# Two-layer hybrid decoder in fp32: the end of the last up unit ahead of the down units' preparation, and other tiles for their raw weights

## The chip, the cores and the metric

The kernel runs on one core of one Trainium2 chip. The metric is the device time of one execution, in microseconds. The core's engines are named as the profile names them: PE is TensorE (matmuls), PEld its weight loads, DVE is VectorE, ACT is ScalarE, POOL is GpSimd, SP is the engine whose queue issues the weight loads.

## The reference

Activations are 512 tokens by 1024 features; the feed-forward part is 2816 wide (22 chunks of 128).

```
def swiglu(x, w_gate, w_up, w_down):
    return (jax.nn.silu(x @ w_gate) * (x @ w_up)) @ w_down

h = x
for i in range(2):
    # layer 0: h = h + conformer_conv(rms_norm(h));  layer 1: h = h + diff_attention(rms_norm(h))
    u = rms_norm(h, ffn_norm_g[i])
    h = h + swiglu(u, ffn_w_gate[i], ffn_w_up[i], ffn_w_down[i])
    gate = jax.nn.sigmoid(rms_norm(h, ple_norm_g[i]) @ ple_w_gate[i])
    h = h + gate * (p[i] @ ple_w_proj[i])
return h
```

## The kernel before

Everything is kept transposed: `h[c]` holds feature chunk c (128 partitions) for the 512 tokens. Each fp32 product is made of three matmuls on rounded parts (`mm3`: L166 low times high, L167 high times high, L168 high times low). So each operand is split: ScalarE casts it to its high part, VectorE subtracts that from it for the low part. Weights come by DMA on SP's queue into a raw tile and are split in the same way.

The feed-forward function `ffn` goes through its 22 hidden chunks in three parts (6, 8, 8). In the second and third part the gate, up and down products are done by units (`Unit`, with `Gate`, `Up`, `Down`): a unit makes a 256-wide piece of output with seven products of half size instead of eight, each product `p(i)` being 12 matmuls 256 wide. For it a unit needs two raw weight tiles (`load`), sums and differences of their quarters on GpSimd (in `prep(1)`: L739, L740; in `prep(3)`: L751, L752), and their splits (`two`: cast L729, low part L730; the third sum: L755, L756). `drain` takes finished accumulators: L784, L790 and L795 add them up, L816 and L821 multiply up by gate, and L823 and L824 split the hidden chunk into the tile `B{chunk}`. `run` goes through a list of units: while unit n multiplies, unit n+1 is loaded and prepared.

The last eight hidden chunks go through `down`. Output chunks 0 and 1 are done plainly (512-wide matmuls into two accumulators, all chunks one after another), output chunks 2 to 7 by three `Down` units 0, 1, 2. These need differences of the hidden chunks as second operands. They are made out of the up units' results (L830 to L833: on GpSimd, for the last up unit on VectorE) into the tiles C and D, which otherwise hold `pp`, the projected per-layer input, and are split by `sums(k)` (L927 cast, L928 low part). When they have been read, `back` loads `pp` into these tiles again (L954). `add` (L920) adds a finished accumulator to `h`; when a chunk of `h` is finished, `after.chunk(m)` prepares the next norm: split (L206 on ScalarE, L207 on VectorE), square (L225, L228), sum of squares on GpSimd (L229). The gate after it (`ple`) needs the sum over partitions (L199, on TensorE), an inverse root, and its spreading by a matmul (L291) and copy (L262); then L1020 multiplies the gate's accumulator by it, which frees that accumulator.

The order on each engine is set by a tile scheduler that builds the program: it knows the data that each instruction needs and where a tile's buffer comes free, and `tc.issue_after` adds that an instruction is put behind a given one. Tiles are named by tag and count of buffers: `sb([P, 2, S], "A4", 1)` is the one buffer A4, "wraw" has two buffers. A tile with the same tag can be written only when the one before is no longer read.

In a Down unit before the change, raw tiles of unit 0 are in A4, A5, of unit 1 in A6, A7, of unit 2 in "wraw"; its sums are in A2, A3, A4, the third sum in "wth".

Of the kernel before, what the change touches and what calls it, by code (L numbers as in the profile page):

```python
# [15 lines left out]
ALU = mybir.AluOpType  # L16
# [4 lines left out]
P = 128  # L21
S = 512
# [69 lines left out]
def trunk(ctx, tc, xT, pT, wts, diag, dww, vec, rel, onehot, lamv, out):  # L92
    nc = tc.nc
# [45 lines left out]
    t = tp()  # L139
# [69 lines left out]
    class Norm:  # L209


        def __init__(self, g, acc_engine=None):
            self.g, self.u = g, {}
            self.eng = acc_engine or G
# [592 lines left out]
    class Up(Unit):  # L807
# [4 lines left out]
        def ready(self, j, k):  # L812
            o, g = self.out[j], self.gate.out[j]
            cut = slice(k * HT, (k + 1) * HT)
            if j == 1:
                V.tensor_tensor(o[:, cut], self.a[:, :HT] if k == 0 else o[:, cut], g[:, cut], ALU.mult)  # L816
            self.done[j] += 1
            if self.done[j] < 2:
                return
            if j == 0:  # L820
                V.tensor_tensor(o, o, g, ALU.mult)  # L821
            hid = both(sb([P, 2, S], f"B{self.at + j}", 1, F32R))
            A.copy(hid[0], o)  # L823
            V.tensor_tensor(hid[1], o, f(hid[0]), ALU.subtract)  # L824
            self.hid[self.at + j] = hid
            if self.pp and self.done == [2, 2]:
                (u11, u12), (u21, u22) = ((u[:, :HT], u[:, HT:]) for u in self.out)
                t = [x[:, i * HT : (i + 1) * HT] for x in self.pp[self.at : self.at + 2] for i in range(2)]
                eng = G if self.at + 2 < len(self.hid) else V
                eng.tensor_tensor(t[0], u12, u11, ALU.subtract)  # L830
                eng.tensor_tensor(t[1], u22, t[0], ALU.subtract)
                eng.tensor_tensor(t[2], u22, u12, ALU.subtract)
                eng.tensor_tensor(t[3], u21, t[1], ALU.subtract)  # L833

    class Down(Unit):
        def __init__(self, n, m, b, add, done):
            super().__init__(n, False, None)
            self.m, self.b, self.add, self.done = m, b, add, done

        def load(self):  # L840
            self.raw = []
            for j in range(2):
                raw = sb([P, 2, S], *(("wraw", 2) if self.n == 2 else (f"A{4 + 2 * self.n + j}", 1)))
                nc.sync.dma_start(raw, wts[self.i + j].rearrange("p (j k) -> p j k", j=2))
                self.raw.append(raw)
            self.sums = sb([P, 2, S], f"A{2 + self.n}", 1)
            self.s3 = sb([P, S], "wth", 2)

        def third(self):
            return sb([P, S], "wtl", 2, F32R), sb([P, S], "bias", 2, F32R)  # L850
# [14 lines left out]
    def ffn(norm, after, spare, pp, pps):  # L865
# [11 lines left out]
                x.b = ops.at  # L877
            return us

        def run(us, between=lambda: None):  # L880
            for n, x in enumerate(us):
                if n == len(us) - 1:
                    between()
                last = us[n - 1] if n else None
                nxt = us[n + 1] if n + 1 < len(us) else None
                x.start()
                if nxt:
                    nxt.load()
                x.p(1)
                if nxt:  # L890
                    nxt.prep(0)
                x.p(2)
                if nxt:
                    nxt.prep(1)
                if last:
                    last.p(4)
                x.p(6)
                if nxt:
                    nxt.prep(2)
                if last:  # L900
                    last.p(3)
                x.p(5)
                if nxt:
                    nxt.prep(3)
                    nxt.prep(4)
                x.p(7)
                if nxt:
                    nxt.prep(5)
            us[-1].p(4)
            us[-1].p(3)  # L910

        def down(hid):

            ws = [weight(), weight()]
            b = {n: [None] * 4 for n in ("T1", "T2", "T3", "T4")}
# [3 lines left out]
            def add(m, cut, src):  # L919
                V.tensor_tensor(h[m][:, cut], src, h[m][:, cut], ALU.add)  # L920

            def sums(k):
                hi, lo = ops.tiles[k]
                for i in range(2):
                    two = slice(2 * i, 2 * i + 2)
                    src = pp[2 * k + i].rearrange("p (j t) -> p j t", j=2)
                    A.copy(hi[:, two], src)  # L927
                    V.tensor_tensor(lo[:, two], src, f(hi[:, two]), ALU.subtract)  # L928
                for i in range(4):
                    b[f"T{i + 1}"][k] = hi[:, i], lo[:, i]  # L930

            xs = [Down(i, 2 * i + 2, b, add, after.chunk) for i in range(3)]
            x = xs[0]
            x.load()
            x.prep(0)
            x.prep(1)
            for k in range(3):
                sums(k)
            x.prep(3)
            sums(3)  # L940
            x.prep(2)
            x.prep(4)
            accs = mm(), mm()
            for k in range(NC):
                for w_, a_ in zip(ws, accs):
                    mm3(a_, wpart(w_, k), hid[k], k == 0, k == NC - 1)
            for m in range(2):
                add(m, slice(0, S), accs[m])
                after.chunk(m)
            x.prep(5)  # L950

            def back():
                for m in range(NC):
                    nc.sync.dma_start(pp[m], pps[m])  # L954

            run(xs, back)

        us = None
        for at, (f0, n) in enumerate(PARTS):
# [42 lines left out]
            if hooks:  # L1002
                linear(n, hid, add, 2, at=hooks)
                wnext[0] = end
            else:
                down(hid)

    def ple(norm, pp, after, last_cuts=1):
        def sums(m, cuts=1):
# [504 lines left out]
```

## Time and profile before

| | us |
|---|---|
| median of 3 runs | 1272.56 (1271.6 to 1272.82) |
| the profiled execution | 1272.05 |
| its span | 1270.3 |
| layer 0's last up unit and first down unit | about 490 to 536 in the span |
| layer 1's | about 1147 to 1193 |
| the gate after each | begins with L199 at 575.5, and its first accumulator is freed at 585.7 and 1243.5 |

In a row of the timeline stand the start in the span, the time of the instruction, its engine, its line, what it writes and reads by tags, and its shape; in brackets, how long the engine had been idle before and what ended that. Matmuls overlap, so their pitch is the difference of two starts. In the rows of windows stand, for a stretch, its length and the busy time of PE, PEld, DVE, ACT and POOL with the counts, then the granted clock of TensorE (1 is full), the share of the DMA engines that is busy, and GB/s.

### The profile page before, as it was taken

How to read it: one execution, taken by the hardware profiler on the slowest of the kernel's cores; microseconds unless marked ns; L12 is line 12 of the kernel's file. 1: busy time of each engine (PE TensorE's matmuls, PEld its weight loads, DVE VectorE, ACT ScalarE, POOL GpSimd, SP SyncE). 2: the span in 40 equal slices, each digit the busy share in tenths (PEclk: the TensorE clock that was granted, in tenths of full speed). 3: DMA queues.
4: the chain of work that ended last, by engine and by line, in shares of the span. 5: the costliest groups of instructions: out<-in, count | busy, mean ns of one | idle time of the engine just before them, and what ended most of it. 6: DMA issues, size and time to landing. Idle time of an engine off the chain costs nothing.

```text
span 1270.3 us, 19093 instructions
## 1 busy us (share of the span) xinstructions
PE 1239.8 (98%) x7296; PEld 1092.9 (86%) x7296; DVE 937.8 (74%) x1308; ACT 639.3 (50%) x1124; POOL 544.6 (43%) x403
## 2 busy tenths in 40 slices
PE   9999999999999999799999999999999999999798
PEld 7888778889998999697788888888889998999787
DVE  6997866975895488877676876647956984597866
ACT  6652554533553355344666877644434542455332
POOL 3862432025550577523346635141035541696330
PEclk9999999999999999899999999999999999999799
DMA  7556323333333234234442331343243233234132
GB/s 263 187 202 190 125 87 112 92 108 116 100 98 119 83 101 129 87 93 142 125 126 78 101 101 58 102 132 99 83 133 100 88 113 116 84 100 151 50 98 85
DMA packets 53768, 144.79 MB, mean 114 GB/s; under 512 B 6147, under 2 KB 10755, under 8 KB 53676
## 3 DMA queue, kind: packets, MB, share of 16 engines
q1 hardware_dynamic: 50400, 138.04, 34.9%
q10 hardware_dynamic: 3276, 5.53, 1.4%
q8 instruction: 57, 0.93, 0.3%
q14 instruction: 35, 0.29, 0.1%
HBM read 133.04 MB, written 10.51 MB: 113 GB/s over the span
## 4 chain that ended last, share of the span: by engine, by line
PE 81%; DVE 9%; issue 3%; DMA 1%; ACT 1%; SPq 0%; POOL 0%; ACTq 0%; DVEq 0%
PE mm L166 25%; PE mm L168 25%; PE mm L167 25%; DVE wlo L730 2%; PE mm L1225 1%; DVE sc L458 1%; DVE B L824 1%; DVE C L928 1%; PE sc L1193 1%; PE sc L1192 1%; PE tp L1212 1%; PE sc L407 1%; DVE wk L816 1%; PE mm L407 1%; PE mm L363 1%
## 5 line engine op out<-in xcount | busy, mean ns | idle before, releaser
L159 ACT CAST whi<-wraw 128x1024 fp32r<-128x1024 f32 (+2 forms) x133 | 133.1, 1009 | 185.6 <-PE mm L168 71.8
L166 PE MATMUL mm<-A,wlo 128*128 128x512 f32 (+1 forms) x568 | 220.4, 389 | 2.4 <-DVE big L1020 1.9
L167 PE MATMUL mm<-A,whi 128*128 128x512 f32 (+1 forms) x568 | 218.9, 387 | 0.0
L168 PE MATMUL mm<-A,whi 128*128 128x512 f32 (+1 forms) x568 | 217.3, 389 | 0.0
L161 DVE TENSOR_TENSOR wlo<-wraw,whi 128x1024 fp32r<-128x1024 f32 (+2 forms) x129 | 167.6, 1304 | 61.3 <-ACT whi L159 58.8
L166 PE MATMUL mm<-C,wlo 128*128 128x256 f32 x520 | 147.9, 285 | 1.9 <-DVE h L920 1.9
L167 PE MATMUL mm<-C,whi 128*128 128x256 f32 x520 | 147.7, 284 | 0.0
L168 PE MATMUL mm<-C,whi 128*128 128x256 f32 x520 | 147.7, 284 | 0.0
L730 DVE TENSOR_TENSOR wlo<-A,whi 128x1024 fp32r<-128x1024 f32 x74 | 123.2, 1672 | 19.8 <-ACT whi L729 19.3
L166 PE MATMUL mm<-B,wlo 128*128 128x512 f32 (+1 forms) x328 | 123.1, 375 | 12.0 <-ACT B L823 8.3
L166 PEld LDWEIGHTS mm<-A,wlo 128*128 128x128 f32 x568 | 106.8, 188 | 26.3 <-DVE big L1020 2.7
L168 PEld LDWEIGHTS mm<-A,whi 128*128 128x128 f32 x568 | 106.4, 188 | 22.1 <-DVE A L620 0.7
L167 PEld LDWEIGHTS mm<-A,whi 128*128 128x128 f32 x568 | 106.9, 188 | 21.0
L168 PE MATMUL mm<-B,whi 128*128 128x512 f32 (+1 forms) x328 | 120.8, 374 | 1.8 <-DVE B L824 1.8
L167 PE MATMUL mm<-B,whi 128*128 128x512 f32 (+1 forms) x328 | 122.5, 373 | 0.0
L229 POOL TENSOR_TENSOR acc<-acc,wk 128x512 f32<-128x512 f32 x35 | 55.4, 1584 | 151.1 <-ACT wk L228 150.5
L729 ACT CAST whi<-A 128x1024 fp32r<-128x1024 f32 x74 | 77.3, 1048 | 67.4 <-PE mm L168 51.8
L739 POOL TENSOR_TENSOR A<-A 128x512 f32<-128x512 f32 x20 | 31.2, 1560 | 172.6 <-DMA A<-in_wts 171.9
L166 PEld LDWEIGHTS mm<-C,wlo 128*128 128x128 f32 x520 | 100.3, 193 | 3.0 <-DVE h L920 2.7
L167 PEld LDWEIGHTS mm<-C,whi 128*128 128x128 f32 x520 | 100.3, 193 | 0.2
L168 PEld LDWEIGHTS mm<-C,whi 128*128 128x128 f32 x520 | 100.3, 193 | 0.0
L739 POOL TENSOR_TENSOR A<-wraw 128x512 f32<-128x512 f32 x18 | 30.8, 1709 | 149.3 <-DMA wraw<-in_wts 139.8
(341 smaller groups left out, 3196.9 us busy)
## 6 DMA issues: line engine op xcount, KB each, us to landing
wraw<-in_wts SPq DMA_DIRECT2D x153, 512.0 KB, 3.6
A<-in_wts SPq DMA_DIRECT2D x40, 512.0 KB, 3.5
wraw<-in_wts SPq DMA_DIRECT2D x16, 384.0 KB, 3.1
D<-in_diag SPq DMA_DIRECT2D x22, 256.0 KB, 4.9
C<-in_diag SPq DMA_DIRECT2D x16, 256.0 KB, 4.8
C<-pp SPq DMA_DIRECT2D x10, 256.0 KB, 2.6
h<-in_xT SPq DMA_DIRECT2D x8, 256.0 KB, 5.1
rest<-h SPq DMA_DIRECT2D x8, 256.0 KB, 2.0
```

The costliest lines, as they stand in the source:

```text
L159: A.copy(hi[:, cut], raw[:, cut])
L161: eng.tensor_tensor(lo[:, cut], raw[:, cut], f(hi[:, cut]), ALU.subtract)
L166: T.matmul(acc, al, bh, start=first, stop=False, **kw)
L167: T.matmul(acc, ah, bh, start=False, stop=False, **kw)
L168: return T.matmul(acc, ah, bl, start=False, stop=last, **kw)
L229: self.last = self.eng.tensor_tensor(self.acc, self.acc, sq, ALU.add)
L363: last_tap[0] = T.matmul(acc, dg[:, j % 4], ups[c][:, j : j + S], start=(j == 0), stop=(j == PE_TAPS[c] - 1))
L407: last_tap[0] = T.matmul(acc[:, g * P : (g + 1) * P], w, ups[c][:, g, LEAD - m : LEAD - m + P], start=(m == 0), stop=(m == LAGS - 1),)
L458: last_v_tap[0] = V.scalar_tensor_tensor(sum_, tap(j), wt(c, j), sum_, ALU.mult, ALU.add)
L729: A.copy(hi, src)
L730: V.tensor_tensor(lo, src, f(hi), ALU.subtract)
L739: G.tensor_tensor(s[:, 0], r1[:, 0], r1[:, 1], ALU.add)
```

## The change

`Up.ready` keeps the cast and the subtraction of the last hidden chunk as `ends`, and `down` puts most of its own preparation behind them: the differences' splits of the last half chunks (`sums(k, 1)` and `sums(3, 0)`), `prep(2)`, `prep(4)`, `prep(5)`. `sums` is cut into halves for that; `prep(1)` and `prep(3)` come ahead of `prep(0)`. Units 0 and 1 have their raw tiles in A0, A1, unit 2 in A4, A5, whose two loads are put behind the load before; the sums are in A2, A3, A6, the third sum in A6, A7, A7. The norm's chunks 0 and 1 are called when unit 1 begins and no longer ahead of unit 0.

```diff
-            A.copy(hid[0], o)
-            V.tensor_tensor(hid[1], o, f(hid[0]), ALU.subtract)
+            self.ends = A.copy(hid[0], o), V.tensor_tensor(hid[1], o, f(hid[0]), ALU.subtract)
...
-                raw = sb([P, 2, S], *(("wraw", 2) if self.n == 2 else (f"A{4 + 2 * self.n + j}", 1)))
-                nc.sync.dma_start(raw, wts[self.i + j].rearrange("p (j k) -> p j k", j=2))
+                raw = sb([P, 2, S], f"A{4 * (self.n == 2) + j}", 1)
+                with tc.issue_after(self.ahead[0].ins) if self.n == 2 else nullcontext():
+                    self.ahead[0] = nc.sync.dma_start(raw, wts[self.i + j].rearrange("p (j k) -> p j k", j=2))
                 self.raw.append(raw)
-            self.sums = sb([P, 2, S], f"A{2 + self.n}", 1)
-            self.s3 = sb([P, S], "wth", 2)
+            self.sums = sb([P, 2, S], f"A{(2, 3, 6)[self.n]}", 1)
+            self.s3 = sb([P, 2, S], f"A{(6, 7, 7)[self.n]}", 1)[:, 0]
...
-        def down(hid):
+        def down(hid, ends):
...
-            def sums(k):
+            def sums(k, i):
                 hi, lo = ops.tiles[k]
-                for i in range(2):
-                    two = slice(2 * i, 2 * i + 2)
...
+                two = slice(2 * i, 2 * i + 2)
...
+            def behind():
+                both_ = ExitStack()
+                for i in ends:
+                    both_.enter_context(tc.issue_after(i.ins))
+                return both_
...
             x.load()
+            x.prep(1)
+            x.prep(3)
             x.prep(0)
-            x.prep(1)
             for k in range(3):
-                sums(k)
-            x.prep(3)
-            sums(3)
-            x.prep(2)
-            x.prep(4)
+                sums(k, 0)
+            with behind():
+                sums(3, 0)
+                x.prep(2)
+                for k in range(4):
+                    sums(k, 1)
+                x.prep(4)
...
             for m in range(2):
                 add(m, slice(0, S), accs[m])
-                after.chunk(m)
-            x.prep(5)
+            with behind():
+                x.prep(5)
...
+            def behind_first():
+                for m in range(2):
+                    after.chunk(m)
+
-            run(xs, back)
+            run(xs, (lambda: None, behind_first, back))
...
-                down(hid)
+                down(hid, us[-1].ends)
```

The lines below the edit get other numbers: the hidden chunk's low part is L823 (L824 before), the differences L829 to L832 (L830 to L833), the down units' loads L845 (L844), the add L921 (L920), the reloads L964 (L954), the gate's multiplication L1034 (L1020). L928 keeps its number.

What this moves is seen in the order of the engines. First VectorE at the end of layer 0's last up unit, before: `wk_4665` and `wk_4666` are that unit's results, B_744 and B_745 its hidden chunks, C_362 to C_421 are halves of the differences' splits, `wlo_4842` a split of unit 0.

```order
L816 TENSOR_TENSOR wk_4666<-mm_4667,big_4533 128x256
L756 TENSOR_TENSOR bias_4846<-wth_4816,wtl_4845 128x512
L928 TENSOR_TENSOR C_378_2051<-D_237_1295,C_377_2050 128x512
L928 TENSOR_TENSOR C_405_2210<-D_255_1380,C_404_2209 128x512
L795 TENSOR_TENSOR wk_4665<-wk_4665,mm_4668 128x256
L824 TENSOR_TENSOR B_744_4775<-wk_4666,B_744_4775 128x512
L730 TENSOR_TENSOR wlo_4842<-A_754_4815,whi_4841 128x1024
L821 TENSOR_TENSOR wk_4665<-wk_4665,big_4532 128x512
L756 TENSOR_TENSOR bias_4988<-wth_4921,wtl_4987 128x512
L830 TENSOR_TENSOR C_264_1423<-wk_4665 128x256
L832 TENSOR_TENSOR C_264_1423<-wk_4666,wk_4665 128x256
L824 TENSOR_TENSOR B_745_4792<-wk_4665,B_745_4792 128x512
```

And the same place after:

```order
L816 TENSOR_TENSOR wk_4666<-mm_4667,big_4533 128x256
L823 TENSOR_TENSOR B_744_4775<-wk_4666,B_744_4775 128x512
L795 TENSOR_TENSOR wk_4665<-wk_4665,mm_4668 128x256
L821 TENSOR_TENSOR wk_4665<-wk_4665,big_4532 128x512
L829 TENSOR_TENSOR C_264_1423<-wk_4665 128x256
L831 TENSOR_TENSOR C_264_1423<-wk_4666,wk_4665 128x256
L830 TENSOR_TENSOR C_264_1423<-wk_4666,C_264_1423 128x256
L823 TENSOR_TENSOR B_745_4792<-wk_4665,B_745_4792 128x512
L832 TENSOR_TENSOR C_264_1423<-wk_4666,C_264_1423 128x256
L730 TENSOR_TENSOR wlo_4834<-A_754_4815,whi_4833 128x1024
L928 TENSOR_TENSOR C_362_1963<-D_233_1275,C_361_1962 128x512
L928 TENSOR_TENSOR C_378_2051<-D_237_1295,C_377_2050 128x512
```

The multiplication and the splits of both hidden chunks now stand in one row, and the down unit's split and the halves of the sums stand behind them; two third sums (L756) and a sum that stood between are also behind.

Second, SP's queue from the first loads of the down units on, before: A_770, A_771 are unit 1's raw tiles, A_752, A_753 unit 0's, wraw_5009, wraw_5011 unit 2's; wraw_4799 and wraw_4805 are the plain weights, and the D and C rows are the reloads of `pp`.

```order
L844 DMA A_770_4916<-in_wts 128x1024
L844 DMA A_771_4918<-in_wts 128x1024
L155 DMA wraw_4799<-in_wts 128x1024
L844 DMA A_752_4811<-in_wts 128x1024
L155 DMA wraw_4805<-in_wts 128x1024
L844 DMA wraw_5009<-in_wts 128x1024
L844 DMA wraw_5011<-in_wts 128x1024
L844 DMA A_753_4813<-in_wts 128x1024
L954 DMA D_231_1265<-pp_1220 128x512
```

After, from the gate's two weights on (unit 0's A_752, A_753 and the plain weights stand ahead of them); here A_766, A_767 are unit 1's raw tiles and A_784 the first of unit 2's.

```order
L155 DMA wraw_5339<-in_wts 128x1024
L964 DMA D_231_1265<-pp_1220 128x512
L964 DMA D_235_1285<-pp_1222 128x512
L964 DMA D_239_1305<-pp_1224 128x512
L845 DMA A_766_4905<-in_wts 128x1024
L964 DMA D_233_1275<-pp_1221 128x512
L964 DMA D_237_1295<-pp_1223 128x512
L964 DMA D_255_1380<-pp_1225 128x512
L964 DMA C_264_1423<-pp_1226 128x512
L964 DMA C_264_1423<-pp_1227 128x512
L845 DMA A_767_4907<-in_wts 128x1024
L845 DMA A_784_5009<-in_wts 128x1024
```

Units 1 and 2 had all their raw tiles ahead of the reloads; now unit 1's second stands behind the last of them, and unit 2's behind that. On GpSimd unit 0's four operations (L739, L751, L740, L752) move ahead of the last GpSimd differences of the up units, where they stood among those of units 1 and 2, and the eight operations of units 1 and 2 move behind the first L229 of the norm.

Third, TensorE in the gate after the down units, around the column sum of the squares, before: mm_5297, mm_5345 and mm_5402 are the accumulators of the gate's first three chunks.

```order
L168 MATMUL mm_5297<-A_810_5285,whi_5292 128x512
L166 MATMUL mm_5297<-A_808_5266,wlo_5293 128x512
L167 MATMUL mm_5297<-A_808_5266,whi_5292 128x512
L168 MATMUL mm_5297<-A_808_5266,whi_5292 128x512
L199 MATMUL tp_5322<-ones_70,acc_4903 128x128 x4
L168 MATMUL mm_5345<-A_810_5285,whi_5340 128x512
L166 MATMUL mm_5345<-A_808_5266,wlo_5341 128x512
```

And after, where mm_5444 is the fourth accumulator of the gate:

```order
L166 MATMUL mm_5444<-A_792_5062,wlo_5440 128x512
L167 MATMUL mm_5444<-A_792_5062,whi_5439 128x512
L168 MATMUL mm_5297<-A_810_5285,whi_5292 128x512
L166 MATMUL mm_5297<-A_808_5266,wlo_5293 128x512
L167 MATMUL mm_5297<-A_808_5266,whi_5292 128x512
L168 MATMUL mm_5297<-A_808_5266,whi_5292 128x512
L199 MATMUL tp_5322<-ones_70,acc_5001 128x128 x4
L168 MATMUL mm_5345<-A_810_5285,whi_5340 128x512
```

Eleven matmuls of mm_5444 and two others now stand ahead of L199, so 13 rows more. Between L199 and the first L291 there are 31 rows before and 21 after; the second L291 stood two rows ahead of the next accumulator's first matmul and now stands right before it.

## What I predict

> **What bounds the kernel now.** I read the page first.
>
> ```profile
> span 1270.3 us, 19093 instructions
> PE 1239.8 (98%) x7296; PEld 1092.9 (86%) x7296; DVE 937.8 (74%) x1308; ACT 639.3 (50%) x1124; POOL 544.6 (43%) x403
> ```
>
> TensorE is busy 98% of the span, so a change that keeps its work pays only by what it waits or runs slowly. The edited place comes twice, once a layer, and I asked what TensorE waits for between 455 and 700 us (layer 0: seconds in all, times, longest).
>
> ```profile
> PE mm L166 <- ACT B L823: 4.1, 1, 4.1
> PE mm L166 <- DVE wk L795: 1.6, 1, 1.6
> PE mm L166 <- DVE h L920: 1.0, 1, 1.0
> PE mm L166 <- DVE big L1020: 0.9, 1, 0.9
> PE mm L168 <- DVE B L824: 0.9, 1, 0.9
> PE mm L166 <- DVE wlo L730: 0.6, 1, 0.6
> ```
>
> All but the fourth stand at the seam between the last up unit and the first down unit. TensorE's timeline there, and the granted clock of three stretches (PE, weight load, DVE, ACT, POOL busy; clock; DMA; the last is layer 1's seam, 1181.73 less 524.94 = 656.79 us later):
>
> ```profile
> 512.71 0.28 PE L166 MATMUL mm<-wth,wlo 128*128 128x256 f32 x1
> 517.17 0.28 PE L168 MATMUL mm<-B,whi 128*128 128x256 f32 x1
> 519.05 0.38 PE L166 MATMUL mm<-B,wlo 128*128 128x256 f32 x1 [1.61 <-DVE wk L795]
> 524.94 0.79 PE L166 MATMUL mm<-B,wlo 128*128 128x512 f32 x1 [4.15 <-ACT B L823]
> 533.12 0.39 PE L166 MATMUL mm<-C,wlo 128*128 128x256 f32 x1 [1.02 <-DVE h L920]
> 535.39 0.39 PE L166 MATMUL mm<-B,wlo 128*128 128x256 f32 x1 [0.57 <-DVE wlo L730]
> 517.30:524.94 7.64, 1.89 (x15) 1.54 (x13) 7.64 (x6) 0.62 (x1) 7.56 (x5) 1.00 0.25 69
> 524.94:531.75 6.81, 5.94 (x14) 4.58 (x15) 5.67 (x9) 1.91 (x3) 2.02 (x2) 0.50 0.09 23
> 1174.10:1181.73 7.63, 1.92 (x14) 1.54 (x12) 7.63 (x6) 0.62 (x1) 7.55 (x5) 0.90 0.25 71
> ```
>
> From 517.29 to 535.39, 18.1 us, it has 12 matmuls 256 wide, 12 of 512, 3 and 12 more of 256. At full clock matmuls start .12 and .2275 us apart (512.71 to 517.17 is 21 narrow and 9 wide ones), so this is 27 x .12 + 12 x .2275 = 5.97 us of work: 12.1 us are lost per layer, 8.2 in the five waits, the rest at the clock of 0.50. Why they arise stands on VectorE and ScalarE:
>
> ```profile
> 520.27 2.29 DVE L730 TENSOR_TENSOR wlo<-A,whi 128x1024 fp32r<-128x1024 f32 x1
> 522.49 1.74 DVE L821 TENSOR_TENSOR wk<-wk,big 128x512 f32<-128x512 f32 x1
> 524.15 1.75 DVE L756 TENSOR_TENSOR bias<-wth,wtl 128x512 fp32r<-128x512 f32 x1
> 525.83 1.49 DVE L830 TENSOR_TENSOR C<-wk 128x256 f32<-128x256 f32 x1
> 524.26 0.62 ACT L823 CAST B<-wk 128x512 fp32r<-128x512 f32 x1 [7.17 <-DVE wk L821]
> 538.76 0.74 DVE L207 SCALAR_TENSOR_TENSOR A<-h,vec,A 128x512 fp32r<-128x512 f32 x1
> 542.00 0.42 DVE L920 TENSOR_TENSOR h<-mm,h 128x256 f32<-128x256 f32 x1
> 542.34 1.22 DVE L730 TENSOR_TENSOR wlo<-wraw,whi 128x1024 fp32r<-128x1024 f32 x1
> 543.47 0.69 DVE L756 TENSOR_TENSOR bias<-wth,wtl 128x512 fp32r<-128x512 f32 x1
> 544.07 0.75 DVE L920 TENSOR_TENSOR h<-mm,h 128x256 f32<-128x256 f32 x2
> ```
>
> VectorE takes sums and weight splits of the down units ahead of L821, the last hidden chunk; ScalarE waits 7.17 us for it and TensorE for ScalarE. The last four rows give pitches without GpSimd at work: .34 (256 wide), 1.13 (1024), .60 (512); L207 takes .66. The first four, with GpSimd busy 7.56 of 7.64 us, give 2.22, 1.66, 1.68 for 1.13, .60, .60: each VectorE operation on two SBUF operands waits about 1.07 us more, which I call a turn. Additions that read an accumulator (.34) show none.
>
> **The change part by part.** No instruction is added or removed; it moves some. The cuts of the sums into halves, the printed line numbers and the list for `between` cost nothing by themselves.
>
> *One: unit 0's four GpSimd operations come early* (about four of 1.3 to 1.7 us, by the rows below), because its raw weights in A0, A1 land early. They fill GpSimd's idle time ahead of L830's work, and VectorE's splits beside them take turns.
>
> ```profile
> 495.78 1.65 POOL L830 TENSOR_TENSOR D<-wk 128x256 f32<-128x256 f32 x1 [4.60 <-DVE wk L821]
> 510.49 1.28 POOL L739 TENSOR_TENSOR A<-A 128x512 f32<-128x512 f32 x1 [5.99 <-DMA A<-in_wts]
> 499.59 0.41 DVE L790 TENSOR_TENSOR big<-big,mm 128x256 f32<-128x256 f32 x1
> 500.81 0.28 PE L166 MATMUL mm<-wth,wlo 128*128 128x256 f32 x1
> ```
>
> Two to three turns, 2.1 to 3.2 us, push L790, which frees the accumulator for the product at 500.81; it has .8 us of room (500.81 less 500.00). Lost: 1.3 with two, 2.4 with three; I take 1.3, since L790 itself reads an accumulator and only the two splits (L730) ahead of it stand beside the moved work for their whole length. POOL's idle 5.99 at 510 shrinks for it, and that work is gone from the seam.
>
> *Two: the seam.* VectorE now goes straight on from the product that ends at about 512.9 (the row at 512.71): L816 to 513.24; the cast, .6, to 513.95; its low part to 514.55; L795 514.9; L821 515.5; cast to 516.2 beside three u-differences; low part 517.2; the last difference 517.54. TensorE finds accumulator and hidden chunks ready: the waits on L795, L823 and L824 go. What is late next are VectorE's delayed rows: a split (1.13), three halves of sums (1.8), third (.6), a sum, an add, a sum, an add (2.4), the 256-wide add (.34): 6.27, until 523.8. GpSimd has nothing of unit 0 left, so no turns are counted. TensorE is there at 517.29 + 1.44 + 2.73 + .36 = 521.82 and waits 2.0; then 12 x .12. VectorE's next splits take 1.13, one turn beside L229 and 1.13, to 527.2: a second wait of 1.9. TensorE begins unit 1 at 527.2 instead of 535.39: 8.2 earlier, 6.9 with part one.
>
> *Three: the later units' loads.* Unit 1's second raw tile uses A1, whose last reader is VectorE's split of A_753 at 524.94, and stands on SP behind the two C reloads; unit 2's two loads stand behind it. A load lands in 3.5 us:
>
> ```profile
> A<-in_wts SPq DMA_DIRECT2D x40, 512.0 KB, 3.5
> 552.77 0.28 PE L166 MATMUL mm<-C,wlo 128*128 128x256 f32 x1
> ```
>
> So it is there at 528.5, not some 20 us ahead. The first three GpSimd operations of unit 1 end at 528.5 + 3 x 1.3 = 532.4; and VectorE, in order, stands at L756 until its cast is done: 531.8. Queued behind are unit 1's and 2's splits, the moved norm splits, and the adds which free TensorE's accumulators. Up to the add that the product at 552.77 waits for they are 5 x 1.13 + 2 x .60 + 3 x .66 + 8 x .34 = 11.55 us: 543.4 with no turn, and 552.0 with eight (GpSimd has its eight operations of both units and the norm's in the same 20 us). TensorE could be there at 527.2 + 144 x .12 = 544.5. I take six turns, nearer to the upper end since in the rows at 520 each of three in a row took one: 549.8, 551.1 with part one, against 552.77. Of the 6.9 us gained 1.7 are left; 5.2 went into new small waits on L921 and L730.
>
> *Four: into the gate.* The column sum L199 of the norm comes 13 matmuls (2.96 us) later in TensorE's order, the two of L291 stand right before the product that waits for the gate's first add.
>
> ```profile
> 575.51 1.05 PE L199 MATMUL tp<-ones,acc 128*128 128x128 f32 x8
> 576.83 1.22 DVE L161 TENSOR_TENSOR wlo<-wraw,whi 128x1024 fp32r<-128x1024 f32 x1
> 581.82 1.05 ACT L159 CAST whi<-wraw 128x1024 fp32r<-128x1024 f32 x1 [3.20 <-DMA wraw<-in_wts]
> 584.32 0.59 ACT L262 COPY rb<-tp 128x512 f32<-128x512 f32 x1 [1.45 <-PE tp L291]
> 584.94 2.48 DVE L1020 TENSOR_TENSOR big<-mm,rb 128x512 f32<-128x512 f32 x4 [0.81 <-ACT rb L262]
> 585.69 0.50 PE L166 MATMUL mm<-A,wlo 128*128 128x512 f32 x1 [0.95 <-DVE big L1020]
> 1243.46 0.50 PE L166 MATMUL mm<-A,wlo 128*128 128x512 f32 x1 [0.95 <-DVE big L1020]
> ```
>
> L199 at 575.51 - 1.7 + 2.96 = 576.8, 1.3 later. From it runs a chain: VectorE's first operation after it, the split that frees a raw tile, the load, ScalarE's cast (now 583.1 to 584.2), its copy (to 584.9; its 1.45 us of room are used up), VectorE's split behind that cast, the gate's add, TensorE. It resumes at about 586.2 against 585.69: +.5, after idling some 3.2 us instead of .95. So all the gain of the seam is given back there.
>
> *Sum.* Layer 0: +.5. Layer 1: +.5, less what the old seam's half clock cost it beyond layer 0: 1243.46 - 585.69 - 656.79 = .98. Together 0.0.
>
> *The clock.* A wait of 3.2 us may cost it. In layer 1's seam the mean of 0.90 over 7.63 us is 1.5 us at half, so the clock fell 1.5 us before the restart at 1181.73, some 2.7 us into the wait; at 519.05, after 1.61 us, it did not fall. A drop costs at most half a stretch like 524.94 to 531.75, 3.4 us, or 1.6 if half of it lies over waits. Two places, each with half a chance and 2.3 between: +2.3. [...]
>
> The profiled execution took 1272.05 us, its span 1270.3 and 1.75 around it; the median of the runs is 0.5 higher. I add 2.3 to the first and get 1274.4, as a median about 1274.5. A measurement here tells about 0.2%, 2.5 us, from no change.
>
> **The rivals.** *The turns are all taken (slower).* All eight turns instead of six give 2 x 1.07 x 2 layers = 4.3 above the 1274.4: 1278.7. With six and the clock down at both gates it is 1272.05 + 4.6 = 1276.7. Middle: 1277.5. For it: VectorE lost a turn at each of three operations in a row. Against: adds from accumulators show none. It decides from seven turns.
>
> *The turns fall beside waits (faster).* If the eight cost nothing, VectorE is done at 543.4, before TensorE's 544.5, and no later wait arises: L199 comes 5.2 us earlier than I put it, 571.6, and the gate resumes at 581, 4.7 before 585.69. Then 1272.05 - 9.4 - 1.0 + 2.3 = 1264. For it: VectorE has idle time while A_767 is loaded. Against: that idle time comes before the raw tile, the turns after. It takes under four turns to get past 0.2%.
>
> *The clock holds at the gate.* The sum stays at 0.0: 1272 to 1272.5. For it: the .95 and 1.61 us waits left the clock at full. [...]
>
> **How the numbers follow.** Nearly all given back with one drop or so, 1274.5: .36. Clock holds, 1272.3: .12. Turns or clock worse, 1277.5: .32. Turns hidden, 1264 to 1268: .20. So faster by over 0.2% .20, within .48, slower .32. The range goes from 1266, halfway into the turns-hidden case, to 1280, past all eight turns with one clock drop half paid.
>
> **What would show it.** Right: TensorE has no wait on L795 or L823 at the seam; new waits on L921 and L730 within 30 us of it; a wait of about 1.3 on L790 at 501; GpSimd's L739 waits for the A load until about 528; a wait of about 3 us at the gate on L1034 (L1020 before), twice, with PEclk at 0.50 behind one of them. Wrong: no waits between 530 and 552 (turns were cheap), the gate's wait still about 1 us (the chain from L199 has room I missed), or a stretch at half clock at the seam itself.

## The result, and the profile after

The changed kernel took 1276.17 us in the median of 10 runs (1275.01 to 1277.71), the kernel before 1272.13 us beside it (1271.36 to 1274.94): a ratio of 1.0031, with a 95% interval of 1.0021 to 1.0041. It is slower by 4.0 us. The forecast was 1274.5 in a range of 1266 to 1280, with "within 0.2%" as the likeliest and "slower by over 0.2%" at .32. The range holds, the likeliest case does not.

The page's first lines after, and what TensorE waits for between 490 and 600 us (seconds in all, times, longest):

```profile
span 1275.0 us, 19093 instructions
PE 1239.9 (97%) x7296; PEld 1092.5 (86%) x7296; DVE 932.8 (73%) x1308; ACT 639.1 (50%) x1124; POOL 549.7 (43%) x403
PE mm L166 <- DVE h L921: 5.0, 4, 2.1
PE mm L166 <- DVE big L1034: 2.8, 1, 2.8
PE mm L166 <- DVE wlo L730: 1.6, 2, 1.4
PE mm L166 <- DVE big L790: 1.3, 1, 1.3
```

TensorE's busy time is the same. The waits of 4.1, 1.6 and .9 us on L823, L795 and L824 are gone; in their place stand L921 and L730 behind the seam, 1.3 us on L790 ahead of it, and at the gate 2.8 us where there were .9. In time, layer 0 (with L199, and unit 1's first product at 528.88) and the two places of layer 1 that tell the most:

```profile
503.15 0.39 PE L166 MATMUL mm<-wth,wlo 128*128 128x256 f32 x1 [1.32 <-DVE big L790]
526.62 0.39 PE L166 MATMUL mm<-C,wlo 128*128 128x256 f32 x1 [2.14 <-DVE h L921]
528.88 0.58 PE L166 MATMUL mm<-B,wlo 128*128 128x256 f32 x1
536.42 0.39 PE L166 MATMUL mm<-C,wlo 128*128 128x256 f32 x1 [0.75 <-DVE h L921]
538.32 0.39 PE L166 MATMUL mm<-C,wlo 128*128 128x256 f32 x1 [0.20 <-DVE wlo L730]
545.75 0.39 PE L166 MATMUL mm<-B,wlo 128*128 128x256 f32 x1 [1.43 <-DVE wlo L730]
550.09 0.39 PE L166 MATMUL mm<-C,wlo 128*128 128x256 f32 x1 [1.20 <-DVE h L921]
552.69 0.38 PE L166 MATMUL mm<-C,wlo 128*128 128x256 f32 x1 [0.91 <-DVE h L921]
578.50 1.05 PE L199 MATMUL tp<-ones,acc 128*128 128x128 f32 x8
587.54 0.50 PE L166 MATMUL mm<-A,wlo 128*128 128x512 f32 x1 [2.77 <-DVE big L1034]
1162.51 0.39 PE L166 MATMUL mm<-wth,wlo 128*128 128x256 f32 x1 [1.31 <-DVE big L790]
1246.54 0.50 PE L166 MATMUL mm<-A,wlo 128*128 128x512 f32 x1 [2.88 <-DVE big L1034]
```

The five waits of layer 0 from 536 on add up to .75 + .20 + 1.43 + 1.20 + .91 = 4.49 us. A wait in brackets counts from the modelled end of the matmul before, and TensorE loses more by it than that. So the two profiles are compared by the start of the same matmul, the one in the same place of TensorE's order. Where nothing has moved yet the difference is .61 us (497.81 before, 498.42 here), and it is taken off for layer 0. The second matmul of the product behind L790 starts at 500.93 before and at 503.38 here: 2.45, so 1.84 us are lost at that place, not 1.32. In layer 1 the difference is 3.13 ahead of the place (1154.64, 1157.77) and 4.97 behind it (1157.76, 1162.73): 1.84 again.

What holds the gate is seen on ScalarE and VectorE. And behind both gates the clock is down (the column behind POOL's count):

```profile
584.59 1.04 ACT L159 CAST whi<-wraw 128x1024 fp32r<-128x1024 f32 x1 [2.98 <-PE tp L291]
585.54 0.58 ACT L262 COPY rb<-tp 128x512 f32<-128x512 f32 x1
585.66 1.23 DVE L161 TENSOR_TENSOR wlo<-wraw,whi 128x1024 fp32r<-128x1024 f32 x1 [1.00 <-ACT whi L159]
586.81 2.48 DVE L1034 TENSOR_TENSOR big<-mm,rb 128x512 f32<-128x512 f32 x4
587.50:594.00 6.50, 6.46 (x21) 5.20 (x22) 4.63 (x7) 4.52 (x6) 0.00 (x0) 0.74 0.48 137
1246.54:1253.00 6.46, 6.46 (x21) 5.20 (x22) 5.64 (x9) 4.52 (x6) 0.00 (x0) 0.74 0.03 8
```

The copy that the gate needs stands behind a cast of a later weight, and the gate's first multiplication behind that weight's split. The row puts the end of the cast's wait down to L291, whose first matmul ended about then; the cast's load had only just landed too: its last packets moved until 584.2 and the cast began .4 later, as in the profile before (581.4 and 581.82, there put down to the load). At a mean clock of 0.74 over 6.50 and 6.46 us, 1.69 and 1.68 us of TensorE are lost.

### The profile page after: what moved, and what is told of

It reads as the page before. It is cut to its first block, busy times and chain, and to the rows that moved or that the text cites. A ratio compares the mean times of both kernels' runs of the same rounds, so it can differ in the third digit from the quotient of the medians.

```text
span 1275.0 us, 19093 instructions
## 1 busy us (share of the span) xinstructions
PE 1239.9 (97%) x7296; PEld 1092.5 (86%) x7296; DVE 932.8 (73%) x1308; ACT 639.1 (50%) x1124; POOL 549.7 (43%) x403
## 4 chain that ended last, share of the span: by engine, by line
PE 74%; DVE 11%; issue 4%; POOL 3%; DMA 3%; ACT 2%; SPq 1%; ACTq 0%; DVEq 0%; POOLq 0%
PE mm L166 23%; PE mm L167 22%; PE mm L168 22%; DVE wlo L730 2%; PE mm L1239 1%; DVE sc L458 1%; DVE wlo L161 1%; DMA A<-in_wts 1%; DMA wraw<-in_wts 1%; POOL A L739 1%; PE sc L1207 1%; PE sc L1206 1%; POOL A L752 1%; DVE A L207 1%; PE tp L1226 1%
## 5 line engine op out<-in xcount | busy, mean ns | idle before, releaser
L730 DVE TENSOR_TENSOR wlo<-A,whi 128x1024 fp32r<-128x1024 f32 x78 | 132.0, 1700 | 19.7 <-ACT whi L729 19.1
L229 POOL TENSOR_TENSOR acc<-acc,wk 128x512 f32<-128x512 f32 x35 | 61.4, 1754 | 167.6 <-ACT wk L228 167.0
L167 PE MATMUL mm<-B,whi 128*128 128x512 f32 (+1 forms) x328 | 120.4, 367 | 0.0
L168 PE MATMUL mm<-B,whi 128*128 128x512 f32 (+1 forms) x328 | 118.7, 367 | 0.0
L729 ACT CAST whi<-A 128x1024 fp32r<-128x1024 f32 x78 | 81.4, 1047 | 60.3 <-PE mm L168 40.3
L739 POOL TENSOR_TENSOR A<-A 128x512 f32<-128x512 f32 x22 | 36.0, 1635 | 163.4 <-DMA A<-in_wts 162.0
L739 POOL TENSOR_TENSOR A<-wraw 128x512 f32<-128x512 f32 x16 | 25.6, 1600 | 148.9 <-DMA wraw<-in_wts 148.9
```

Source lines behind the costliest of these rows:

```text
L167: T.matmul(acc, ah, bh, start=False, stop=False, **kw)
L168: return T.matmul(acc, ah, bl, start=False, stop=last, **kw)
L229: self.last = self.eng.tensor_tensor(self.acc, self.acc, sq, ALU.add)
L729: A.copy(hi, src)
L730: V.tensor_tensor(lo, src, f(hi), ALU.subtract)
L739: G.tensor_tensor(s[:, 0], r1[:, 0], r1[:, 1], ALU.add)
```

## The experiments

All ratios are to the kernel before on the same chip; each edit is made to the changed kernel except in the ninth run, and the tenth adds to the seventh. The first eight runs were on one chip, the ninth and tenth on another. Beside them the kernel before took 1271.43 to 1272.38 us in the medians, so differences in us to the changed kernel, which are differences of medians, are good to about 1 us. In the diffs, dots stand for code left out. Where an edit adds lines, the numbers behind it shift: L922 and L929 are then L921, L1036 and L1042 are L1034, L731 is L730, L791 and L797 are L790; in the fourth run L920 is L921.

**1. The column sum earlier.** The last matmuls of the gate's accumulators 1 and 2 and all of 3 are put behind L199.

```diff
...
                 for k in range(NC):
+                    late = m == 3 or m in (1, 2) and k == NC - 1
+                    with tc.issue_after(norm.cs.ins) if late else nullcontext():
                         mm3(acc, wpart(w, k), ...)
```

> The changed kernel with one thing pinned: the last matmuls of the gate's second and third accumulator and all of the fourth stand behind the column sum L199, which so comes 9 rows (9 x .2275 = 2.05 us) earlier in TensorE's order. Theory A (the gate's wait hangs on where L199 stands): the gate's wait of 2.8 us shrinks to about .8, the clock stays up behind it (1.7 us less a layer), so 2 x (2.05 + 1.7) = 7.5 us less than the changed kernel, about 1268.7. Theory B (the wait hangs on the weight's load and ScalarE's cast, wherever L199 is): within 1 us of the changed kernel, 1275 to 1277.

1277.0 us, ratio 1.0039 (1.0025 to 1.0052): nothing gained, as theory B has it. Its nine runs spread from 1273.48 to 1280.69, and the profile is of the longest. L199 does come 2.2 us earlier against L790, yet the wait is longer. First two rows of TensorE, then ScalarE:

```profile
575.65 1.05 PE L199 MATMUL tp<-ones,acc 128*128 128x128 f32 x8
587.32 0.80 PE L166 MATMUL mm<-A,wlo 128*128 128x512 f32 x1 [3.35 <-DVE big L1036]
584.36 1.04 ACT L159 CAST whi<-wraw 128x1024 fp32r<-128x1024 f32 x1 [1.91 <-DMA wraw<-in_wts]
585.32 0.58 ACT L262 COPY rb<-tp 128x512 f32<-128x512 f32 x1
```

The scheduler answered the pin by putting one more cast, of the eighth weight, ahead of the copy L262; that cast waits for its load until 584.36, while L291 had ended by 584.0. So this run does not test L199 by itself; it shows that the copy behind a cast is enough to hold the gate.

**2. TensorE kept busy during the wait.** Twelve matmuls with an unused result behind L291.

```diff
...
         rb = norm.rows()
+        with tc.issue_after(last_spread[0].ins):
+            d = sc()
+            for k in range(12):
+                last_d = T.matmul(d, norm.u[7][0][:, :P], norm.u[7][0], start=k == 0, stop=k == 11)
```

> The changed kernel with 12 further matmuls 512 wide (2.73 us of TensorE, results unused) between L291 and the product that waits at the gate. Theory A (the wait of 2.8 us costs the clock, and that 1.7 us a layer, besides its own length): the gate's product starts at the same time within .3 us, the clock stays at 1.00 behind it, 3.4 us less in all, about 1272.8. Theory B (the clock would have fallen for other reasons, or its price is hidden by waits that follow): no change or some tenths more, 1276 to 1277.

1273.43 us, ratio 1.0010 (1.0001 to 1.0019): 2.7 us less than the changed kernel although TensorE does 5.5 us more.

```profile
584.36 2.88 PE L1049 MATMUL sc<-A 128*128 128x512 f32 x12
587.31 0.50 PE L166 MATMUL mm<-A,wlo 128*128 128x512 f32 x1
587.50:594.00 6.50, 6.50 (x29) 5.36 (x29) 4.92 (x8) 5.14 (x7) 0.00 (x0) 1.00 0.54 156
1246.54:1253.00 6.46, 6.42 (x28) 5.35 (x29) 5.65 (x9) 4.53 (x6) 0.00 (x0) 1.00 0.03 10
610.52 0.50 PE L166 MATMUL mm<-whi,A 128*128 128x512 f32 x1 [1.16 <-DVE A L207]
```

The clock is 1.00 behind both gates, 29 and 28 matmuls stand in the stretches that held 21. So the wait costs its length and the clock behind it, as theory A has it; 3.4 us were expected and 2.7 came. A reason why not all came is the last row: with the clock up in layer 0, TensorE waits 1.16 us for L207 at 610.5, a wait that the changed kernel's profile does not have. There the lower clock (0.74 behind the gate) covers it.

**3. Unit 1's raw weights in other tiles,** so that nothing waits for A1.

```diff
-                raw = sb([P, 2, S], f"A{4 * (self.n == 2) + j}", 1)
+                raw = sb([P, 2, S], *(("wraw", 2) if self.n == 1 else (f"A{4 * (self.n == 2) + j}", 1)))
```

> The changed kernel with unit 1's raw weights in the two wraw buffers instead of A0, A1, so that all six raw tiles are loaded ahead of the reloads, as before the change. Theory A (the late loads make the waits after the seam): GpSimd does the eight operations of units 1 and 2 from about 504 to 517; one to three turns of 1.07 us fall on the seam, and the waits between 536 and 553 (4.5 us in layer 0) go: 2 to 4 us less a layer, 1268 to 1272. Theory B (each GpSimd operation costs VectorE a turn wherever it stands, and all turns end on TensorE): the seam's wait grows from 2.1 by what the later waits lose, 1275 to 1277.

1274.65 us, ratio 1.0021 (1.0012 to 1.0030): 1.5 us less than the changed kernel, outside what either theory said, and nearer to B. TensorE, VectorE and GpSimd at the seam:

```profile
530.01 0.58 PE L166 MATMUL mm<-C,wlo 128*128 128x256 f32 x1 [5.40 <-DVE h L921]
526.18 2.85 DVE L928 TENSOR_TENSOR C<-C,C 128x512 fp32r<-128x512 f32 x2
525.14 1.66 POOL L739 TENSOR_TENSOR A<-A 128x512 f32<-128x512 f32 x1 [7.29 <-DVE bias L756]
```

Of the waits behind the seam only .58 us on L730 is left, and the seam's own has grown from 2.14 to 5.40: unit 2's operations on GpSimd wait for a tile until VectorE's L756 and then run beside VectorE's last rows at the seam (2.85 us for two sums of .60). The early load moves the wait.

**4. The tiles and loads of before, the order of the changed kernel.**

```diff
-                raw = sb([P, 2, S], f"A{4 * (self.n == 2) + j}", 1)
-                with tc.issue_after(self.ahead[0].ins) if self.n == 2 else nullcontext():
-                    self.ahead[0] = nc.sync.dma_start(raw, ...)
+                raw = sb([P, 2, S], *(("wraw", 2) if self.n == 2 else (f"A{4 + 2 * self.n + j}", 1)))
+                nc.sync.dma_start(raw, ...)
```

with the sums in A2, A3, A4 and "wth" again.

> The changed kernel with the tiles and loads of the kernel before: the end of the last up unit first, and the norm's two chunks at unit 1, stay. Unit 0's second raw tile is then A5 again and lands late, so all of GpSimd's operations lie beside the seam. Theory A (the order at the seam alone is not enough, turns take its place): the seam's wait grows to 5 to 8 us, the later waits go, 1274 to 1280. Theory B (the order is the gain, the tiles are the loss): the seam as in the changed kernel, later waits gone, 2 x 5 us less than the changed kernel, 1264 to 1268.

1277.41 us, ratio 1.0042 (1.0029 to 1.0054), within theory A. The seam:

```profile
521.49 0.99 PE L168 MATMUL mm<-B,whi 128*128 128x512 f32 x2 [2.48 <-DVE B L823]
530.25 0.58 PE L166 MATMUL mm<-C,wlo 128*128 128x256 f32 x1 [5.00 <-DVE h L920]
```

7.5 us of wait there, and the same 2.9 at the gate: the order and the norm's later place bring nothing without the tiles. The reverse, the tiles without the order or with the norm's chunks in their old place, was not tried: the norm's first chunk would take A0 ahead of unit 1's raw tile and hold it until the gate.

**5. The copy ahead of the cast.**

```diff
...
-            w = weight()
+            w = weight(after=(None, norm.rb_copy if m == 6 else None))
```

> The changed kernel with ScalarE's copy L262 pinned ahead of the cast of the gate's seventh weight, which waits for its load and stood ahead of the copy; L199 stays where it is. Theory A (after the run with the earlier L199: what holds the gate is the copy behind that cast, and VectorE's split behind it): L291 ends at 584.8 in layer 0, copy to 585.4, first L1034 to 586.1, product at 586.1 instead of 587.5; the wait is 1.3 and the clock stays up: 2 x (1.45 + 1.7) less, about 1270. Theory B (the wait hangs on the weights' loads themselves): the product then waits for its weight, 1275 to 1277.

1270.95 us, ratio 0.9992 (0.9983 to 1.0000): 5.2 us less than the changed kernel. One edit at the gate, none at the seam, and all of the loss is gone.

```profile
584.45 0.58 ACT L262 COPY rb<-tp 128x512 f32<-128x512 f32 x1 [3.21 <-PE tp L291]
585.81 0.50 PE L166 MATMUL mm<-A,wlo 128*128 128x512 f32 x1 [1.40 <-DVE big L1034]
```

The wait is 1.40, the clock 1.00 behind it.

**6. Three pins at the gate:** the first run's on L199, the fifth's on the copy, and L291 ahead of the fourth accumulator's last two chunks.

```diff
...
+                    late = m == 3 and k < NC - 2 or m in (1, 2) and k == NC - 1
+                    pin = norm.cs if late else last_spread[0] if m == 3 else None
+                    with tc.issue_after(pin.ins) if pin else nullcontext():
                         mm3(acc, wpart(w, k), ...)
```

> The changed kernel with three pins at the gate: L199 nine rows earlier (as in the first run), L291 ahead of the last two chunks of the fourth accumulator (5 rows earlier), and the copy L262 ahead of the seventh weight's cast. Theory A (the gate's wait is the order of these three, each after the other): no wait, or under .5 us, and the clock at 1.00: 2 x (2.8 + 1.7) = 9 us less than the changed kernel, about 1267, below the kernel before. Theory B (weights or banks bind right behind it): at most 4 us less, 1272 or more.

1267.69 us, ratio 0.9961 (0.9949 to 0.9972). The 8.5 us that it is below the changed kernel are theory A's 9. All of TensorE's waits from 490 to 600 us (the last line is L790 under its number here):

```profile
PE mm L166 <- DVE h L922: 4.9, 4, 2.1
PE mm L166 <- DVE wlo L731: 1.6, 2, 1.4
PE mm L166 <- DVE big L791: 1.3, 1, 1.3
```

The seam's waits are those of the changed kernel; the gate's is gone.

**7. Unit 2's loads do not wait.**

```diff
-                with tc.issue_after(self.ahead[0].ins) if self.n == 2 else nullcontext():
+                with nullcontext():
```

> The changed kernel without the wait that puts unit 2's two loads behind unit 1's; the scheduler then loads them early, and also puts L199 24 rows earlier in TensorE's order and L291 12 to 14 rows earlier, with the copy L262 still behind the seventh cast. Theory A (the gate's wait is a matter of the order at the gate): wait of at most 1 us there, 5 to 8 us less than the changed kernel, 1268 to 1271; the seam and the small waits behind it change by under 1 us a layer. Theory B (the copy behind the cast binds anyway, as with the earlier L199): the wait stays at 2.5 to 3.4, 1275 to 1278.

1265.55 us, ratio 0.9944 (0.9932 to 0.9956), 10.6 us less than the changed kernel, more than theory A said.

```profile
PE mm L166 <- DVE h L921: 4.1, 3, 2.6
PE mm L166 <- DVE wlo L730: 2.5, 3, 1.8
PE mm L166 <- DVE big L790: 1.3, 1, 1.3
570.15 1.05 PE L199 MATMUL tp<-ones,acc 128*128 128x128 f32 x8
```

The waits at and behind the seam are in layer 0 as large as before the edit, 6.6 us each (L921 and L730 together). What went is the gate's: the scheduler now put L199 24 rows earlier. The remaining 2.1 us against the sixth run I can't assign; in this profile the clock at layer 0's seam was 1.00 (526 to 534), in the sixth run's 0.79.

**8. Without GpSimd's sums of units 1 and 2** (their weight sums are replaced by raw tiles, so this leaves out a part of the computation).

```diff
             elif step == 1:
+                if self.skip:
+                    self.sums = r0
+                    return
```

and the like for `prep(3)`, with `skip` set for Down units 1 and 2.

> The changed kernel with GpSimd's eight operations of down units 1 and 2 left out in each layer (their weight sums are replaced by the raw tiles, so the output is not the reference's); loads, splits and matmuls stay. Theory A (of the waits between the seam and 553, most are VectorE's turns beside these operations and the 4 us that they take after the late load): the 4.3 to 5.2 us of small waits behind unit 1's start shrink to under 1.5, 3 us or more less a layer, unless the gate takes it back; 1267 to 1271. Theory B (the late load alone makes the waits): they stay, 1275 to 1277.

1266.45 us, ratio 0.9956 (0.9944 to 0.9968), just below theory A's range. All waits from 490 to 600 us:

```profile
PE mm L166 <- DVE h L929: 2.7, 1, 2.7
PE mm L166 <- DVE big L1042: 2.7, 1, 2.7
PE mm L166 <- DVE big L797: 1.3, 1, 1.3
```

One wait at the seam, one at the gate, and none of the 4.49 us between, though the loads are as late as in the changed kernel. The waits behind the seam hang on GpSimd's eight operations. Whether on their turns or on their own length behind the load is not told apart, since both went. The gate's wait is as long as in the changed kernel, so what is saved ahead of it is not taken back there.

**9. The kernel before, with the sixth run's pins.**

> The kernel before, with the same three pins at the gate (L199, L291, copy L262). Theory A (the gate's order became a loss only with the change, which makes TensorE arrive there earlier against VectorE and ScalarE): only the .95 us of wait at each gate can go, at most 1.9 us, 1270 to 1272. Theory B (the gate's order is a loss of its own that the change only shares): 5 us or more less, 1267 or below.

1270.29 us, ratio 0.9981 (0.9973 to 0.9990): 2.1 us less in the medians, some .2 more than the two waits of .95 hold. So the gate's order cost little before; it is the change that made it dear, as theory A has it. That TensorE arrives at the gate earlier, which theory A gives as the reason, is not what the profiles show: L291 ends at 584.3 before, and at 584.8 less .61 in the changed kernel.

**10. The seventh run's kernel, with unit 0's sums behind the up units' differences on GpSimd.**

```diff
...
+            with tc.issue_after(diff.ins):
                 x.prep(1)
                 x.prep(3)
```

> The version of the seventh run (unit 2's loads not waiting), with GpSimd's four operations of down unit 0 pinned behind the last difference of the third up unit, where VectorE is idle, instead of ahead of them. Theory A (part one of the prediction: these operations cost VectorE turns ahead of L790): the wait of 1.31 us on L790 at the seam goes in both layers and nothing takes its place, 2.6 us less than the seventh run, about 1263. Theory B (the turns go elsewhere, or the operations come too late for the seam's splits): the wait on L921 at the seam grows by as much, 1265 to 1267.

1261.32 us, ratio 0.9910 (0.9894 to 0.9927). The wait on L790 is gone in both layers, and in layer 0 the others stay as in the seventh run:

```profile
PE mm L166 <- DVE h L921: 4.1, 3, 2.6
PE mm L166 <- DVE wlo L730: 2.5, 3, 1.8
```

2.6 us were expected and 4.2 came. Most of the difference is how the wait was counted: by the starts of the same matmuls TensorE loses 1.83 and 1.86 us at L790 in the seventh run, 3.7 in all, and nothing in the tenth. In layer 1 the waits on L921 and L730 also went from 6.9 to 5.1. And the two runs were on different chips, so some tenths may lie there. This is the best version: 11 us below the kernel before and 15 below the changed one.

## Why the prediction was right or wrong

The parts can be followed through layer 0. Forecast is how much later (-: earlier) a matmul should start than before, measured is the difference of its starts less .61.

| the same matmul of layer 0 | before, after | forecast | measured |
|---|---|---|---|
| the product behind L790 (its second matmul) | 500.93, 503.38 | +1.3 | +1.84 |
| unit 1's first product | 535.39, 528.88 | -6.9 | -7.12 |
| the product at 552.77 before | 552.77, 552.69 | -1.7 | -.69 |
| the gate's | 585.69, 587.54 | +.5 | +1.24 |

**Part one** (L790, 1.3 a layer): the waits are 1.32 and 1.31, but TensorE loses 1.84 in each layer. VectorE comes to L790 2.5 us later (502.69 against 499.59, less .61): two L730 and one L821 ahead of it take .78, 1.09 and .66 longer, where the prediction counted two turns, 2.1. The tenth run, in which moving those four operations removes the wait, shows the cause.

**Part two** (the seam): the waits on L795 and L823 went; the first new one was put at 2.0 and is 2.14. The second, 1.9, is not there in this profile. The prediction gave VectorE a turn beside L229; its two splits took 2.35 us, none longer than without GpSimd, and it is L229 that took 3.00:

```profile
526.48 2.35 DVE L730 TENSOR_TENSOR wlo<-A,whi 128x1024 fp32r<-128x1024 f32 x2
```

So unit 1's first product gained 7.12 + 1.84 = 9.0 us on the kernel before, apart from part one, and not 8.2. TensorE ran at a lower clock there (0.79 from 526 to 534), which the prediction had counted among the signs of being wrong. It cost nothing: in the second run's profile the clock stayed up at this place, and the next wait was 2.17 us instead of .75.

**Part three** (5.2 us of the gain back in small waits): 6.4 measured in layer 0 (7.12 less .69), 4.49 of it in the brackets, by an operation chain that was named rightly. GpSimd's first operation of unit 1 waits for its load until 531.69, VectorE for L755:

```profile
531.69 1.29 POOL L739 TENSOR_TENSOR A<-A 128x512 f32<-128x512 f32 x1 [1.73 <-DMA A<-in_wts]
534.92 1.12 DVE L756 TENSOR_TENSOR bias<-A,wtl 128x512 fp32r<-128x512 f32 x1 [3.09 <-ACT wtl L755]
```

The load was expected at 528.5 and came 2.6 us later (less .61), because the split that frees its tile ended at about 527.6 and not at 524.9. On the other side, VectorE's operations from 534.9 to 552 take 4.4 us longer than without GpSimd (six of them, by .44 to 1.09): about four turns, not six. That the part came out as near as it did is therefore partly luck: the one term was put too small, the other too large. The eighth run confirms that these operations carry the waits. The rival that they would cost nothing is out for the changed kernel.

**Part four** (gate): from -1.7 to +.5, 2.2 us, was forecast, and 1.93 measured (-.69 to +1.24). In layer 1 the gate's product starts 3.08 later than before, against 3.13 ahead of the moved work: -.05; the prediction had +.5 - .98 = -.48. The chain was named rightly in its last steps (cast, copy, split, add). Its first was not shown: with L199 earlier the gate did not start earlier, and with the copy ahead of the cast, L199 left where it was, it started 1.7 us earlier (585.81 against 587.54, the start of both profiles being equal to .01). L199 and L291 are worth a further 3.3 us (sixth run less fifth) once the copy is free.

**The sum.** The parts were put at 0.0 for both layers and came to 1.24 - .05 = 1.2: part one was mis-sized by .5 in each layer. The clock was put at 2.3, as two waits of 3.2 us, each with half a chance of 2.3; the waits came out at 2.77 and 2.88, and both drops came in the profile. From the gate of layer 0 to the moved work of layer 1 the difference grows by 1.28 us (1.85 to 3.13), from the gate of layer 1 to the end by 1.61 (3.08 to 4.69). The four terms give 1.24 - .05 + 1.28 + 1.61 = 4.1, and the medians differ by 4.0. In layer 1 the 1.61 is the clock's: in the second and third run, where it stayed up, nothing is lost there. In layer 0 it is not the clock alone: those two lose 1.2 and 1.1 us in the same stretch at full clock, by the wait on L207 at 610.5 and 611.7, which the prediction had put at nothing.

The outcome is near the rival "six turns and the clock down at both gates", put at 1276.7; the likeliest case had one drop. That rival's number was partly luck: it has 4.6 us for the clock and nothing for the parts. The second run shows the price of the clock at both gates: 2.7 us.

The trace shows each of the waits of 2.14, 2.77 and 2.88 us followed by a stretch at half clock (0.50 from 527.27, 588.72 and 1247.49 on, 3.41 us each). So the rival that the clock holds is out for the changed kernel's profile.

What the prediction missed altogether is that the loss was cheap to undo: it took the order at the gate as given, and weighed the waits only as consequences of the loads.

## What to carry to other kernels

When an edit moves work in one stage, follow all engines into the next stage that they all enter. Here L199 came 13 matmuls later while L291 ended at about the same time, so the chain that starts at L199 had 2.5 us less (6.3 instead of 8.8 from L199's start to L291's end), and the copy came to stand behind a cast that waits for a load. Look for the small operation which everyone needs and which stands behind a large one that nobody needs yet; to put it ahead was worth 5 us here, with an edit of two lines. An explicit wait on a load can cost less by its own delay than by what a scheduler makes of it elsewhere, so compare the order of all engines far behind the edit.

## What the runs showed of the hardware

At the gate of the changed kernel the clock fell after the wait, not during it, for waits of 2.77 and 2.88 us. Behind the gate's 2.77 us TensorE's 512-wide matmuls start .23 us apart at first, and from 588.9 on .43 apart: 1.3 us after work had begun again, and until about 591.9. In layer 1 the clock is at 0.50 from 1247.49 on, .95 us after the start at 1246.54.

It is not a matter of the wait's length alone. Behind the seam's wait of 2.14 or 2.15 us in layer 0 the mean clock from 526 to 534 was 0.79 in the profiles of the changed kernel and of the fifth and sixth run, and 1.00 in those of the first and second. The seventh run's 2.62 us there left it at 1.00, and so did the third run's 2.88 us at the gate (587.5 to 594).

In the profile of the kernel before the clock is at 0.50 from 524.92 for 6.83 us and from 1180.28 for 13.65; in that of the changed kernel from 527.27, 588.72, 1186.05 and 1247.49, for 3.41 us each. One more stretch in each, from 1269.02 and 1274.79, runs past the end. The finished ones are one, two and four times 3.41 us long, and within a profile all start a whole number of times 3.41 us apart. From these starts each profile is divided here into steps of 3.41 us. Two steps each at layer 0's gate, first of the changed kernel, then of the third run, whose wait there ends at 588.31; its steps are laid by its own stretch at half clock, three steps from 529.1 to 539.4 (0.69 from 526 to 534, 0.60 from 533 to 541):

```profile
585.31:588.72 3.41, 1.18 (x5) 1.00 (x6) 3.06 (x5) 0.81 (x2) 0.00 (x0) 1.00 0.65 169
588.72:592.13 3.41, 3.41 (x10) 2.66 (x9) 1.79 (x2) 2.74 (x3) 0.00 (x0) 0.50 0.37 143
583.73:587.14 3.41, 1.70 (x8) 1.08 (x6) 2.30 (x3) 1.53 (x2) 0.00 (x0) 1.00 0.40 126
587.14:590.55 3.41, 2.24 (x10) 1.86 (x11) 2.91 (x5) 0.92 (x1) 0.00 (x0) 1.00 0.76 257
```

In the changed kernel 2.23 us of the step are idle (3.41 less 1.18), and the next step is at half. In the third run the longer wait is divided into 1.71 and 1.17, and the clock stays up. In the profiles of the kernel before and the changed kernel, from 20 us on, eight steps at full clock have 2.14 us or more idle, three before and five after, and each is followed by half clock; all other steps at full clock have 1.67 us or less, and none is. The work lost to one such step at the gate was 1.69 and 1.68 us, about half of 3.41.

From this an estimate: if waits of 2.8 us fall anywhere on such steps alike, and if 1.9 us in one step, the middle of 1.67 and 2.14, are enough, (3.41 - 2.8 + 2 x .9) / 3.41 = .7 of them are followed by half clock.
